# A hybrid decoder layer on one core: the triangular inverses multiplied into the keys' and outputs' operands, their rows in place of columns, and another place for the tiles between the chains

## The chip, the cores and the metric

The kernel runs on one core of one Trainium2 chip. The metric is the device time of one execution in microseconds (us). For before it is the median of three runs; the profile is of one further execution. TensorE does the matrix products, VectorE, ScalarE and GpSimd the rest, and SyncE issues most of the loads; each engine works through its own queue in order.

## The reference

One layer of a decoder over 1,024 prompt tokens and 8 x 4 sample tokens, width 1,024, float32. A Conformer convolution and an RWKV-7 time mixing run side by side on the same normed input, are merged by two sigmoid gates, and a gated MLP follows. What the change touches is the time mixing: 16 heads of 64, with the state S of 64 x 64 per head:

```python
def step(S, inp):
    r_t, w_t, k_t, a_t, b_t, v_t = inp
    sa = jnp.einsum('bhij,bhj->bhi', S, a_t)
    S = S * w_t[:, :, None, :] + sa[..., :, None] * b_t[..., None, :] + v_t[..., :, None] * k_t[..., None, :]
    y = jnp.einsum('bhij,bhj->bhi', S, r_t)
    return S, y
...
gates = jax.nn.sigmoid(zg.astype(f32))
m = gates[..., :D_MODEL] * ya.astype(f32) + gates[..., D_MODEL:] * yb.astype(f32)
```

## The kernel before

The kernel runs in four parts: the norm and the first projections (`mixer_a`), the time mixing (`mixer_b`), the merge and the output projection, and the MLP. Every large product is split into a high and a low part, so a tile of a projection is 8 x 3 products for each of three blocks of 352 tokens: 72 products of TensorE, named `mm` in the trace.

`mixer_b` cuts the prompt into chunks of 64 tokens and works on four chunks of four heads at a time, a group n of 16. Each group goes through five steps, each of them a generator:

- `prep(n)` loads keys, decays and values, and `operands(n)` writes the scaled operands E and BK.
- `stage(n)` forms the 64 x 64 lower triangles of the chunks in LQ (columns 0:64 for the inverse, 64:128 for the outputs). It inverts the 32 x 32 diagonal blocks: the blocks go to DRAM (`dL`) and come back as the tile L with one block per partition (four copies), then VectorE does 31 steps of two instructions, a product into `tm` and an addition to `X`; the result goes to DRAM (`dX`) and back into LQ. L, X and `tm` exist once (pool `lanes`).
- `combine(n)` fills the block below the diagonal with two times 16 products of 32 columns.
- `chain(n)` carries the state through its four chunks one after the other. One chunk: TensorE forms R from the state (tile `c`), VectorE copies R, TensorE multiplies by the inverse (U), VectorE scales U by `nin` into UV, TensorE multiplies by the keys BT (X), VectorE adds to the decayed state. The outputs gather in the tile `y`, which ScalarE evicts when the chain is done (`Yev`, L1173).
- `group_norm(n)` norms the outputs.

Beside them run the sample tokens, the convolution's norm (`ln_block`) and the **fillers**: 18 tiles of r, k and v, 16 tiles of gates, and at the end 8 half tiles of the convolution's output. `drive` sets the order of all this before the kernel runs: a clock counts TensorE's work at full speed, each generator yields how long it wants to wait, and while none is due the fillers emit products one by one. A group's chain waits for `combine(n)`, its stage for chain n-2, its operands for chain n-3 (three buffers). A gate is due when five or fewer have been emitted (`GATE0`) or when the chain five places back is done. The convolution's outputs start when the last chain is done (`conv_in` reuses the space of the stages). The tile framework then orders each engine's queue once more by its own schedule.

Of the kernel before, what the change touches and what calls it, by code (L numbers as in the profile page):

```python
# [7 lines left out]
F32 = mybir.dt.float32  # L8
# [23 lines left out]
class Net:  # L32
# [648 lines left out]
    def mixer_b(self):  # L681
# [4 lines left out]
        self.t_stage = {}  # L686
        self.st, self.pr, self.ch = {}, {}, {}
# [62 lines left out]
    def s_chain(self):  # L750
        for n in range(self.NH):
            yield from self.wait(("comb", n))
            yield from self.chain(n)
            self.done.add(("chain", n))
# [101 lines left out]
    GATE0 = 5  # L856

    def fillers(self):
# [5 lines left out]
        while gates or tiles or conv:  # L864
# [3 lines left out]
            if tiles:  # L868
                yield from self.rkv_tile(*tiles.pop(0))
            elif gates and due():  # L870
                yield from self.gate(*gates.pop(0))
                if not gates:
                    self.done.add("gates")
# [137 lines left out]
    def stage(self, n):  # L1011
# [4 lines left out]
        for g in range(2):  # L1016
            c4 = slice(4 * g, 4 * g + 4)
            for x in range(2):
# [7 lines left out]

                nc.gpsimd.memset(LQ[64 * x + 32:64 * x + 64, c4, 0:32], 0.0)
# [16 lines left out]
        for s in range(31):  # L1044
            a, m = s // 4 + 1, 31 - s
            tp = tm[:, :a * m].rearrange("p (a m) -> p a m", m=m)
            nc.vector.tensor_tensor(out=tp, in0=L[:, s:s + 1, s + 1:32].to_broadcast([128, a, m]),  # L1047
                                    in1=X[:, :a, s:s + 1].to_broadcast([128, a, m]), op=ALU.mult)
            nc.vector.tensor_tensor(out=X[:, :a, s + 1:32], in0=X[:, :a, s + 1:32], in1=tp, op=ALU.add)  # L1049
# [28 lines left out]
    def combine(self, n):  # L1078
# [3 lines left out]
        D11 = self.sm.tile([128, 8, 32], F32, tag="D11", name="D11", bufs=1)  # L1082
        Y21 = D11
        for x in range(2):
            nc.vector.transpose(out=D11[64 * x:64 * x + 32], in_=LQ[64 * x:64 * x + 32, :, 0:32])
        ps = self.pw_tile()
        pv = ps[:, 0:256].rearrange("p (c t) -> p c t", t=32)
        for x in range(2):
            p, q = slice(64 * x, 64 * x + 32), slice(64 * x + 32, 64 * x + 64)
            for c in range(8):  # L1090
                self.mm(pv[q, c], LQ[p, c, 32:64], D11[p, c], True, True)
        for x in range(2):
            q = slice(64 * x + 32, 64 * x + 64)
            nc.scalar.activation(out=Y21[q], in_=pv[q], func=AF.Copy)
        yield 1200
        pv = ps[:, 256:512].rearrange("p (c t) -> p c t", t=32)
        for x in range(2):
            p, q = slice(64 * x, 64 * x + 32), slice(64 * x + 32, 64 * x + 64)
            for c in range(8):
                self.mm(pv[p, c], Y21[q, c], LQ[q, c, 32:64], True, True)  # L1100
        for x in range(2):
            p = slice(64 * x, 64 * x + 32)
# [598 lines left out]
```

## Time and profile before

| | us |
|---|---|
| median of three runs | 2529.82 |
| the three runs | 2526.34, 2529.82, 2546.9 |
| the profiled execution | 2521.95 |
| its span, first to last instruction | 2520.3 |

The profile is of one execution. Times within it are us from the start of its span, which is 1.65 us shorter than the execution's own time. The trace records an f32 product as two instructions of TensorE (480 records of R's products for 15 groups of 16), and some records of products are missing, so counts of products below are taken from the built program and times from the trace. A clock of 1.00 is 2.4 GHz, one of 0.50 is 1.2 GHz; a mean between them is a mix of the two.

### The profile page before, as it was taken

The page shows a single profiled execution, that of the slowest core. Times are in us where ns is not written, and L with a number is a line of the kernel's source. Part 1 is how long each engine was busy: PE and PEld are TensorE (multiplying, and loading weights), DVE is VectorE, ACT ScalarE, POOL GpSimd, SP SyncE. Part 2 cuts the span into 40 slices and gives each one's busy share as a digit, 9 for nine tenths or more (in the row PEclk, how much of TensorE's full clock was granted, in tenths as well). Part 3 has the DMA queues.
Part 4 walks back from the last instruction along what each step waited for, and adds up shares of the span by engine and source line. Part 5 has one row for each costly group of instructions (what it writes and reads, how often), then busy time and mean ns, then how long its engine had stood idle before and what let it go on. Part 6 is the DMA issues. An engine that isn't in the chain of part 4 may idle for free.

```text
span 2520.3 us, 41895 instructions
## 1 busy us (share of the span) xinstructions
PE 2341.8 (93%) x16094; PEld 2114.6 (84%) x16094; DVE 1646.8 (65%) x4190; ACT 877.9 (35%) x1748; POOL 263.2 (10%) x562
## 2 busy tenths in 40 slices
PE   6789998987889689889999999999999999999998
PEld 5778886765668567767879999999999999999998
DVE  5999777688787877786862344475555545545556
ACT  4234333344344433543443222333232322223235
POOL 2313311011111111221221100000000000000000
PEclk9989997867679789897999999999999999999999
DMA  4124543243323332434334654431111111111111
GB/s 124 49 75 147 172 131 98 55 108 86 107 58 100 107 106 78 125 85 107 106 83 148 234 167 132 122 125 44 46 41 54 35 51 46 45 48 44 51 52 70
DMA packets 289295, 230.65 MB, mean 92 GB/s; under 512 B 82333, under 2 KB 265271, under 8 KB 288575
## 3 DMA queue, kind: packets, MB, share of 16 engines
q1 hardware_dynamic: 268615, 170.17, 24.3%
q0 software_dynamic: 20480, 57.80, 6.6%
q8 instruction: 127, 2.08, 0.4%
q14 instruction: 73, 0.60, 0.1%
HBM read 157.45 MB, written 70.45 MB: 90 GB/s over the span
## 4 chain that ended last, share of the span: by engine, by line
PE 78%; DVE 12%; DMA 6%; ACT 2%; issue 2%; SPq 1%; DVEq 0%; ACTq 0%; POOLq 0%
PE mm L54 62%; PE w L54 6%; PE c L54 2%; PE y L54 2%; DMA L<-dL 2%; DVE sg L359 2%; PE w L61 2%; DMA dX<-X 2%; DVE X L1049 1%; DVE tm L1047 1%; DVE wlo L49 1%; DMA d_ma<-ga 0%; SPq L1051 0%; DVE E L1030 0%; DVE UV L1162 0%
## 5 line engine op out<-in xcount | busy, mean ns | idle before, releaser
L54 PE MATMUL mm<-hH,whi 128*128 128x352 f32 (+1 forms) x2568 | 875.9, 341 | 14.1 <-DVE bcol L497 12.7
L54 PE MATMUL mm<-hH,wlo 128*128 128x352 f32 (+1 forms) x2568 | 851.9, 333 | 18.6 <-DVE wlo L49 18.6
L54 PE MATMUL mm<-hL,whi 128*128 128x352 f32 (+1 forms) x2568 | 854.2, 333 | 0.2 <-DVE hL L248 0.2
L54 PEld LDWEIGHTS mm<-hH,whi 128*128 128x128 f32 (+1 forms) x2568 | 491.2, 191 | 42.8 <-DVE bcol L497 14.3
L54 PEld LDWEIGHTS mm<-hH,wlo 128*128 128x128 f32 (+1 forms) x2568 | 491.6, 192 | 30.8 <-DVE wlo L49 20.8
L54 PEld LDWEIGHTS mm<-hL,whi 128*128 128x128 f32 (+1 forms) x2568 | 492.6, 192 | 11.0 <-issue 2.2
L48 ACT ACTIVATE whi<-wraw 128x1024 fp32r<-128x1024 f32 (+2 forms) x123 | 126.1, 1025 | 425.6 <-PE mm L54 340.3
L1533 DVE TENSOR_TENSOR u<-mm,rs 128x352 f32<-128x352 f32 x144 | 73.5, 511 | 225.1 <-PE mm L54 225.0
L49 DVE TENSOR_TENSOR wlo<-wraw,whi 128x1024 fp32r<-128x1024 f32 (+2 forms) x123 | 145.4, 1182 | 91.5 <-ACT whi L48 91.4
L359 DVE SCALAR_TENSOR_TENSOR sg<-cu,par,sg 128x1024 f32<-128x1024 f32 x120 | 165.4, 1382 | 1.5
L54 PE MATMUL mm<-fH,whi 128*128 128x352 f32 x504 | 163.4, 324 | 0.0
L54 PE MATMUL mm<-fH,wlo 128*128 128x352 f32 x504 | 162.8, 323 | 0.0
L54 PE MATMUL mm<-fL,whi 128*128 128x352 f32 x504 | 162.7, 323 | 0.0
L1588 DVE TENSOR_TENSOR acc<-mm,acc 128x352 f32<-128x352 f32 x168 | 86.9, 522 | 93.6 <-PE mm L54 93.6
L1563 DVE SCALAR_TENSOR_TENSOR c<-u,par,c 128x1024 f32<-128x1024 f32 x96 | 122.9, 1280 | 7.7 <-ACT c L1559 5.3
L54 PE MATMUL w<-E,BK 64*128 64x128 f32 x512 | 93.2, 332 | 32.4 <-DVE tm L1047 13.1
L54 PEld LDWEIGHTS w<-E,BK 64*128 64x128 f32 x512 | 76.5, 227 | 49.4 <-issue 27.3
L1047 DVE TENSOR_TENSOR tm<-L,X 128x60 f32<-128x60 f32 (+24 forms) x496 | 100.4, 202 | 23.6 <-DMA L<-dL 18.4
L1049 DVE TENSOR_TENSOR X<-X,tm 128x60 f32<-128x60 f32 (+24 forms) x496 | 100.4, 202 | 5.3
L54 PEld LDWEIGHTS mm<-fH,whi 128*128 128x128 f32 x504 | 94.8, 188 | 0.5
L54 PEld LDWEIGHTS mm<-fH,wlo 128*128 128x128 f32 x504 | 95.0, 188 | 0.0
L1122 ACT ACTIVATE SP<-UV,PC 64x64 f32<-64x64 f32 x192 | 64.3, 343 | 87.9 <-DVE UV L1162 78.0
(404 smaller groups left out, 3663.5 us busy)
## 6 DMA issues: line engine op xcount, KB each, us to landing
wraw<-w_in SPq DMA_DIRECT2D x50, 512.0 KB
wraw<-w_up SPq DMA_DIRECT2D x48, 512.0 KB
wraw<-w_down SPq DMA_DIRECT2D x32, 384.0 KB
L<-dL SPq DMA_DIRECT2D x16, 512.0 KB
d_alr<-la POOLq DMA_DIRECT2D x8, 528.0 KB, 3.2
d_cum<-lc POOLq DMA_DIRECT2D x8, 528.0 KB, 3.5
d_gout<-lg POOLq DMA_DIRECT2D x8, 528.0 KB, 4.0
d_k<-k POOLq DMA_DIRECT2D x24, 176.0 KB, 2.9
```

Source lines behind the costliest of these rows:

```text
L48: nc.scalar.activation(out=hi[:, :nk, :m], in_=raw[:, :nk, :m], func=AF.Copy)
L49: (lo_eng or nc.vector).tensor_tensor(out=lo[:, :nk, :m], in0=raw[:, :nk, :m], in1=hi[:, :nk, :m].bitcast(F32), op=ALU.subtract)
L54: self.nc.tensor.matmul(out, l, r, start=start, stop=stop)
L61: self.nc.tensor.transpose(out, x, ident)
L359: nc.vector.scalar_tensor_tensor(out=c[:, 0:TP], in0=u[:, t:t + TP], scalar=self.col("conv_w", t * 4 + i), in1=c[:, 0:TP], op0=ALU.mult, o ...
L1047: nc.vector.tensor_tensor(out=tp, in0=L[:, s:s + 1, s + 1:32].to_broadcast([128, a, m]), in1=X[:, :a, s:s + 1].to_broadcast([128, a, m]), ...
L1049: nc.vector.tensor_tensor(out=X[:, :a, s + 1:32], in0=X[:, :a, s + 1:32], in1=tp, op=ALU.add)
L1122: nc.scalar.activation(out=at(SP, u, x), in_=src(x)[:, u], func=AF.Copy, scale=PC[hs[x], 4 * u + c:4 * u + c + 1])
L1533: nc.vector.tensor_tensor(out=u[:, 2 + t0:2 + t0 + m], in0=p, in1=rs[:, t0:t0 + m], op=ALU.mult)
L1563: nc.vector.scalar_tensor_tensor(out=c[:, 0:TP], in0=u[:, t:t + TP], scalar=wt, in1=c[:, 0:TP], op0=ALU.mult, op1=ALU.add)
L1588: nc.vector.tensor_tensor(out=acc[i][:, s], in0=ps[:, :BW], in1=acc[i][:, s], op=ALU.add)
```

## The change

It has three parts. First, `combine` completes the inverse, multiplies it by `nin` and then multiplies it into the operands: the keys' operand BT and the outputs' half of LQ are replaced by their products with it. The chain copies R straight into UV and goes on to X; U, R0 and the products with `nin` are gone from it. The block above the diagonal is cleared by GpSimd in `combine`, where before GpSimd cleared the one below in `stage`. Second, the inverse is computed from the last row upwards, so that a step reads a column of L (32 elements apart) in place of a row; the number of elements is the same in each step of the mirrored order. Third, gates are always due, and chain n waits until min(4 + 2n, 34) filler tiles have been emitted.

```diff
+        self.filled = 0
...
         for n in range(self.NH):
             yield from self.wait(("comb", n))
+            while self.filled < min(self.FILL[0] + self.FILL[1] * n, 34):
+                yield self.POLL
...
-    GATE0 = 5
+    GATE0 = 16
+    FILL = (4, 2.0)
 
...
             if tiles:
                 yield from self.rkv_tile(*tiles.pop(0))
+                self.filled += 1
             elif gates and due():
                 yield from self.gate(*gates.pop(0))
+                self.filled += 1
...
-                nc.gpsimd.memset(LQ[64 * x + 32:64 * x + 64, c4, 0:32], 0.0)
...
-        for s in range(31):
-            a, m = s // 4 + 1, 31 - s
+
+        for s in range(31, 0, -1):
+            a, m = 8 - s // 4, s
             tp = tm[:, :a * m].rearrange("p (a m) -> p a m", m=m)
-            nc.vector.tensor_tensor(out=tp, in0=L[:, s:s + 1, s + 1:32].to_broadcast([128, a, m]),
-                                    in1=X[:, :a, s:s + 1].to_broadcast([128, a, m]), op=ALU.mult)
-            nc.vector.tensor_tensor(out=X[:, :a, s + 1:32], in0=X[:, :a, s + 1:32], in1=tp, op=ALU.add)
+            nc.vector.tensor_tensor(out=tp, in0=L[:, 0:s, s:s + 1].rearrange("p i o -> p o i").to_broadcast([128, a, m]),
+                                    in1=X[:, 8 - a:8, s:s + 1].to_broadcast([128, a, m]), op=ALU.mult)
+            nc.vector.tensor_tensor(out=X[:, 8 - a:8, 0:s], in0=X[:, 8 - a:8, 0:s], in1=tp, op=ALU.add)
...
-        D11 = self.sm.tile([128, 8, 32], F32, tag="D11", name="D11", bufs=1)
-        Y21 = D11
-        for x in range(2):
-            nc.vector.transpose(out=D11[64 * x:64 * x + 32], in_=LQ[64 * x:64 * x + 32, :, 0:32])
+        nin = self.pr[n][3]
+        hs = [slice(0, 64), slice(64, 128)]
+        lo = [slice(64 * x, 64 * x + 32) for x in range(2)]
+        up = [slice(64 * x + 32, 64 * x + 64) for x in range(2)]
+        D22 = self.sm.tile([128, 8, 32], F32, tag="D22", name="D22", bufs=1)
+        for q in up:
+            nc.vector.transpose(out=D22[q], in_=LQ[q, :, 32:64])
         ps = self.pw_tile()
         pv = ps[:, 0:256].rearrange("p (c t) -> p c t", t=32)
-        for x in range(2):
-            p, q = slice(64 * x, 64 * x + 32), slice(64 * x + 32, 64 * x + 64)
+        for p, q in zip(lo, up):
             for c in range(8):
-                self.mm(pv[q, c], LQ[p, c, 32:64], D11[p, c], True, True)
-        for x in range(2):
-            q = slice(64 * x + 32, 64 * x + 64)
-            nc.scalar.activation(out=Y21[q], in_=pv[q], func=AF.Copy)
-        yield 1200
+                self.mm(pv[q, c], LQ[p, c, 32:64], LQ[p, c, 0:32], True, True)
+        for q in up:
+            nc.scalar.activation(out=LQ[q, :, 0:32], in_=pv[q], func=AF.Copy)
+        for p in lo:
+            nc.gpsimd.memset(LQ[p, :, 32:64], 0.0)
+        yield self.W_COMB[0]
         pv = ps[:, 256:512].rearrange("p (c t) -> p c t", t=32)
-        for x in range(2):
-            p, q = slice(64 * x, 64 * x + 32), slice(64 * x + 32, 64 * x + 64)
+        for q in up:
             for c in range(8):
-                self.mm(pv[p, c], Y21[q, c], LQ[q, c, 32:64], True, True)
-        for x in range(2):
-            p = slice(64 * x, 64 * x + 32)
-            nc.scalar.activation(out=LQ[p, :, 32:64], in_=pv[p], func=AF.Copy)
-        yield 1000
+                self.mm(pv[q, c], D22[q, c], LQ[q, c, 0:32], True, True)
+        for q in up:
+            nc.scalar.activation(out=LQ[q, :, 0:32], in_=pv[q], func=AF.Copy)
+        nc.vector.tensor_tensor(out=LQ[:, :, 0:64], in0=LQ[:, :, 0:64],
+                                in1=nin[:, 0:8].rearrange("p (c o) -> p c o", o=1).to_broadcast([128, 8, 64]), op=ALU.mult)
+        for g in range(2):
+            yield self.W_COMB[1 + g]
+            ps = self.pw_tile()
+            pv = ps.rearrange("p (c t) -> p c t", t=128)
+            for c in range(4):
+                for p in hs:
+                    self.mm(pv[p, c, 0:64], LQ[p, 4 * g + c, 0:64], BT[p, 4 * g + c, p], True, True)
+                    self.mm(pv[p, c, 64:128], LQ[p, 4 * g + c, 0:64], LQ[p, 4 * g + c, 64:128], True, True)
+            for p in hs:
+                nc.scalar.activation(out=BT[p, 4 * g:4 * g + 4, p], in_=pv[p, :, 0:64], func=AF.Copy)
+            nc.scalar.activation(out=LQ[:, 4 * g:4 * g + 4, 64:128], in_=pv[:, :, 64:128], func=AF.Copy)
+        yield self.W_COMB[3]
+
+    W_COMB = (1200, 2000, 500, 1200)
 
...
-        PC, nin = self.pr[n][2:4]
+        PC = self.pr[n][2]
...
-        up = lambda t, c, x: t[hs[x], c:8:4].rearrange("p (u o) -> p u o", o=1).to_broadcast([64, 2, 64])
...
-            R0 = self.sm.tile([128, 128], F32, tag="R0", name="R0")
-            nc.vector.tensor_copy(out=R0, in_=R[:, :128])
             for u, x in ux:
                 self.mm(yo(u, x), E[x][:, 4 * u + c, 64:128], UV[:, 4 * u + c, x], c == u == 0, False)
+
+            for x in range(2):
+                nc.vector.tensor_copy(out=UV[hs[x], c:8:4, x], in_=two(R[:, :128])[hs[x]])
             yield self.LAT[0]
-            U = self.pc_tile()
-            for u, x in ux:
-                self.mm(at(U, u, x), LQ[hs[x], 4 * u + c, 0:64], at(R0, u, x), True, True)
-            for x in range(2):
-                nc.vector.tensor_tensor(out=UV[hs[x], c:8:4, x], in0=two(U[:, :128])[hs[x]], in1=up(nin, c, x), op=ALU.mult)
-            yield self.LAT[1]
             X = self.pc_tile()
             for u, x in ux:
                 self.mm(at(X, u, x), BT[:, 4 * u + c, hs[x]], UV[:, 4 * u + c, x], True, True)
...
             for u, x in ux:
...
-                yield self.LAT[2]
+                yield self.LAT[1]
...
-    LAT = (950, 1050, 1200)
+    LAT = (1200, 1500)
```

The change moves nearly everything in `mixer_b`. Two places are shown.

TensorE's queue at the end of the last chain. `c` and `y` are the chain's products, `mm<-hH` and `mm<-hL` products of a gate tile, `mm<-cs` products of the convolution's output. Before:

```order
L54 MATMUL mm<-hL,whi 128x352
L54 MATMUL mm<-hH,wlo 128x352
L54 MATMUL mm<-hH,whi 128x352
L54 MATMUL y<-UV,LQ 64x64
L54 MATMUL mm<-hL,whi 128x352
L54 MATMUL c<-UV,BK 64x64 x4
L54 MATMUL y<-UV,LQ 64x64 x3
L54 MATMUL mm<-hH,wlo 128x352
L54 MATMUL mm<-hH,whi 128x352
L54 MATMUL mm<-hL,whi 128x352
L61 MATMUL w<-ident,Sf 64x128
L54 MATMUL mm<-hH,wlo 128x352
```

After:

```order
L54 MATMUL c<-UV,E_12893 64x64
L54 MATMUL c<-UV,E_12894 64x64
L54 MATMUL c<-UV,E_12893 64x64
L54 MATMUL c<-UV,E_12894 64x64
L54 MATMUL y<-UV,E_12894 64x64
L54 MATMUL y<-UV,LQ 64x64
L54 MATMUL c<-UV,BK 64x64 x4
L54 MATMUL y<-UV,LQ 64x64 x3
L61 MATMUL w<-ident,Sf 64x128 x2
L54 MATMUL mm<-csH,whi 128x352
L54 MATMUL mm<-csL,whi 128x352
L54 MATMUL mm<-csH,wlo 128x352
```

The gate's products stand between the last chain's products and behind it before; after, the last chain's products stand alone, and the convolution's outputs follow them at once.

VectorE's queue within a chain, with the steps of another group's inverse (`tm`, `X`) between its instructions. `R<-c` and `UV<-c` are the chain's, `E` those of `operands`. Before, with the transposition of a `combine` (L1085):

```order
L1143 COPY R_6617<-c 128x128
L1047 TENSOR_TENSOR tm<-L,X 128x72
L1085 STREAM_TRANSPOSE D_6637<-LQ 32x256
L1049 TENSOR_TENSOR X<-X,tm 128x4x18
L1151 TENSOR_TENSOR UV<-c,nin 64x2x64
L1047 TENSOR_TENSOR tm<-L,X 128x68
L1151 TENSOR_TENSOR UV<-c,nin 64x2x64
L1049 TENSOR_TENSOR X<-X,tm 128x4x17
L1275 TENSOR_TENSOR sQK<-w,ms 128x64
L1047 TENSOR_TENSOR tm<-L,X 128x64
L999 TENSOR_TENSOR E_6725<-kn,P 64x8x64
```

After, with the product of LQ and `nin` of a `combine` (L1110), which waits for ScalarE and GpSimd:

```order
L1054 TENSOR_TENSOR X<-X,tm 128x6x11
L1177 SCALAR_TENSOR_TENSOR UV<-c,PC,SP 64x64
L1052 TENSOR_TENSOR tm<-L,X 128x60
L1177 SCALAR_TENSOR_TENSOR UV<-c,PC,SP 64x64
L1054 TENSOR_TENSOR X<-X,tm 128x6x10
L1110 TENSOR_TENSOR LQ<-LQ,nin 128x8x64
L1052 TENSOR_TENSOR tm<-L,X 128x54
L1166 COPY UV<-c 64x2x64
L1054 TENSOR_TENSOR X<-X,tm 128x6x9
L1166 COPY UV<-c 64x2x64
L1052 TENSOR_TENSOR tm<-L,X 128x48
L1005 TENSOR_TENSOR E_9367<-kn,P 64x8x64
```

The chain's step R (a copy) and U (two products with `nin`) has become two copies; the product with `nin` stands once per group between the steps of the inverse.

## Rows read from the trace of the kernel before

**Rows 1.** The page: busy time by engine, and three lines of the forty slices (63 us each; tenths of busy time, and of full clock).

```profile
PE 2341.8 (93%) x16094; PEld 2114.6 (84%) x16094; DVE 1646.8 (65%) x4190; ACT 877.9 (35%) x1748; POOL 263.2 (10%) x562
...
PE   6789998987889689889999999999999999999998
...
DVE  5999777688787877786862344475555545545556
...
PEclk9989997867679789897999999999999999999999
```

**Rows 2.** The instruction that evicts a chain's outputs when the chain is done (line 1173): durations least, median and most in ns, start of the first and the last.

```profile
L1173 ACT ACTIVATE Yev<-y x16: 597/597/602, 452.1 to 1321.1; 128x512 f32<-128x512 f32 x16
```

**Rows 3.** Windows of core 0: the stretch, its length, busy us and instructions of each engine, the granted clock, the DMA share and GB/s. The first is the stretch from the end of chain 0 to that of chain 15, the next seven run from one chain's end to the next one's, the last two are other stretches.

```profile
452.70:1321.70 869.00, 760.00 (x6329) 606.41 (x6329) 658.48 (x2427) 358.20 (x845) 123.97 (x267) 0.83 0.35 94
508.70:579.80 71.10, 58.76 (x453) 48.25 (x452) 54.28 (x197) 30.55 (x73) 7.76 (x21) 0.67 0.49 120
700.20:744.60 44.40, 38.46 (x361) 30.42 (x359) 38.75 (x153) 17.20 (x44) 3.30 (x8) 0.75 0.29 74
794.80:839.70 44.90, 44.90 (x353) 36.68 (x351) 35.85 (x107) 26.03 (x62) 4.76 (x12) 1.00 0.27 79
839.70:957.10 117.40, 86.60 (x583) 69.77 (x582) 91.41 (x339) 39.92 (x88) 16.75 (x38) 0.78 0.41 111
1111.70:1194.90 83.20, 73.22 (x545) 56.27 (x545) 56.25 (x199) 26.05 (x63) 11.70 (x24) 0.77 0.37 99
1194.90:1246.10 51.20, 50.63 (x488) 40.64 (x487) 41.09 (x159) 22.20 (x55) 8.01 (x16) 1.00 0.31 88
1246.10:1290.00 43.90, 43.87 (x391) 34.23 (x390) 32.76 (x126) 20.29 (x47) 13.13 (x22) 1.00 0.52 129
925.00:955.00 30.00, 30.00 (x243) 23.72 (x241) 22.52 (x89) 11.64 (x27) 4.17 (x7) 0.96 0.45 131
1404.00:1454.00 50.00, 46.35 (x281) 45.54 (x280) 26.37 (x39) 14.24 (x17) 4.26 (x8) 0.97 0.81 273
```

**Rows 4.** The inverse: its two instructions as groups of the page, the load of L and the products as the view of one line shows them (durations in ns, first and last start), and forms of the product (busy us, mean ns of one, idle time before).

```profile
L1047 DVE TENSOR_TENSOR tm<-L,X 128x60 f32<-128x60 f32 (+24 forms) x496 | 100.4, 202 | 23.6 <-DMA L<-dL 18.4
L1049 DVE TENSOR_TENSOR X<-X,tm 128x60 f32<-128x60 f32 (+24 forms) x496 | 100.4, 202 | 5.3
...
L1040 SPq DMA_DIRECT2D L<-dL x16: 557/562/617, 348.6 to 1238.5; - x16
...
L1047 DVE TENSOR_TENSOR tm<-L,X x496: 123/206/240, 358.8 to 1279.0; 128x60 f32<-128x60 f32 x16, 128x28 f32<-128x28 f32 x12, 128x66 f32<-128x66 f32 x11, 128x48 f32<-128x48 f32 x10
...
L1047 DVE TENSOR_TENSOR tm<-L,X 128x66 f32<-128x66 f32 x32 | 7.1, 222 | 0.6
...
L1047 DVE TENSOR_TENSOR tm<-L,X 128x29 f32<-128x29 f32 x16 | 2.8, 178 | 0.1
...
L1047 DVE TENSOR_TENSOR tm<-L,X 128x16 f32<-128x16 f32 x16 | 2.7, 166 | 0.2
...
L1047 DVE TENSOR_TENSOR tm<-L,X 128x8 f32<-128x8 f32 x16 | 2.6, 163 | 0.2
```

**Rows 5.** VectorE in order of time (start, us, instruction, idle time before it): the last step of an inverse and the first of the next, at two places.

```profile
766.57 0.17 DVE L1049 TENSOR_TENSOR X<-X,tm 128x8 f32<-128x8 f32 x1
...
854.93 0.19 DVE L1047 TENSOR_TENSOR tm<-L,X 128x31 f32<-128x31 f32 x1 [6.06 <-DMA L<-dL]
...
1051.37 0.17 DVE L1049 TENSOR_TENSOR X<-X,tm 128x8 f32<-128x8 f32 x1
...
1092.01 0.19 DVE L1047 TENSOR_TENSOR tm<-L,X 128x31 f32<-128x31 f32 x1 [2.89 <-DMA L<-dL]
```

**Rows 6.** Pieces of the chain that ended last, in order of time: start, us, what.

```profile
844.01 10.90 DMA L<-dL
...
893.75 10.67 DMA L<-dL
...
929.62 0.38 PE c L54 x8
...
1321.14 4.98 DMA cs<-d_cs
...
1453.26 91.98 PE mm L54 x576
```

**Rows 7.** ScalarE in order of time behind the last chain: the first instruction of the weights of four gate tiles, 1343.72 being the first and 1377.98 the fourth.

```profile
1343.72 1.06 ACT L48 ACTIVATE whi<-wraw 128x1024 fp32r<-128x1024 f32 x1 [3.22 <-DMA wraw<-w_in]
...
1377.98 1.06 ACT L48 ACTIVATE whi<-wraw 128x1024 fp32r<-128x1024 f32 x1 [3.14 <-PE mm L54]
```

**Rows 8.** Groups of instructions from 452 to 1322 us, each shape apart: busy us, mean ns of one, idle time before, and what ended it.

```profile
L1151 DVE TENSOR_TENSOR UV<-c,nin 64x128 f32<-64x128 f32 x120 | 34.4, 287 | 30.8 <-PE c L54 27.8 <-ACT whi L48 0.7
...
L1074 ACT ACTIVATE UV<-w 64x256 f32<-64x256 f32 x56 | 21.2, 378 | 10.7 <-PE w L61 9.9
...
L1143 DVE COPY R<-c 128x128 f32<-128x128 f32 x60 | 17.3, 289 | 41.0 <-PE c L54 40.4
...
L1236 DVE TENSOR_TENSOR Yev<-Yev,mu 128x512 f32<-128x512 f32 x15 | 10.2, 681 | 0.0
```

**Rows 9.** Waits from 452 to 1322 us: engine and line, who ended the wait, us in total, times, longest.

```profile
DVE R L1143 <- PE c L54: 40.4, 27, 5.5
DVE UV L1151 <- PE c L54: 27.8, 29, 6.7
...
POOL LQ L1027 <- DVE LQ L1024: 145.0, 43, 9.9
```


## The prediction

> **What bounds the kernel now.** I read the page's first two parts, then the same stretches by window, then who waited for whom, and last the forms of the instructions that the change touches. The page shows TensorE busy for 93% of the span and VectorE for 65%, and one region where that is not so: from about 340 to 1320 us many slices of TensorE fall to 6 to 8 tenths and its granted clock to 6 to 8 tenths, while VectorE stands at 6 to 8 [rows 1]. This is `mixer_b`. The sixteen chains end between 452.7 and 1321.7 us, 869 us for fifteen intervals, 57.9 us each [rows 2]. In this region TensorE is busy for 760.0 us at a mean clock of 0.83, VectorE for 658.5, ScalarE for 358.2 [rows 3]. So TensorE stands still for 109 us, and a mean of 0.83 of two levels, 2.4 and 1.2 GHz, means the lower one for a third of the time.
>
> The windows from chain end to chain end show why. Where much filler work stands between two chains (the windows that end at 839.7, 1246.1 and 1290.0), TensorE is busy throughout at a clock of 1.00 and an interval takes 43.9 to 51.2 us. Where little does (744.6), or where the next inverse is late (957.1, 1194.9), it takes 44 to 117 us at a clock of 0.75 to 0.78 [rows 3].
>
> What sets the pace there is VectorE. One inverse is 62 instructions, 200.8 us over 16 inverses, 12.55 us each [rows 4], and its buffer L exists once: the next load of L waits for the last step, and the next inverse can't start before that load has landed. The loads are issued every (1238.5 - 348.6)/15 = 59.3 us [rows 4], which is the chains' 57.9. Two of the gaps between inverses are long: 766.6 to 854.9 us and 1051.4 to 1092.0 us [rows 5]. A load takes 10.7 to 10.9 us [rows 6].
>
> Behind the last chain the order of before holds 490 filler products (6.8 gate tiles), and TensorE does them alone, with nothing else to do, at a clock of 1.00: a tile of 72 products takes (1377.98 - 1343.72)/3 = 11.42 us, 0.159 us a product [rows 7]. Then come the convolution's outputs, and the tail starts at 1453.3 us [rows 6].
>
> **The change part by part.** I make the sum against the profiled execution, 2521.95 us; the median of the three runs shown, 2529.82, lies 8 us above it.
>
> *a) The tiles in the order.* Counted in the two built orders, the products of tiles between the end of chain 0 and the end of chain 15 rise from 1612 to 2101, and those between chain 15 and the convolution's outputs fall from 490 to 0. That stretch lasts 1453.3 - 1321.7 = 131.6 us now. What stays of it is the convolution's part, 50 us (1404 to 1454 [rows 3]), and the load of its operand, which the gates hide now and nothing hides then: 4.98 us [rows 6] plus some 3 us for the split and the first product. 131.6 - 58 = **-74 us**. Bounds: -82 if the load is hidden after all, -64 if the 50 us begin at half clock and with both loads late.
>
> The 490 products themselves go among the chains. They cost 490 x 0.159 = 78 us of TensorE at full clock. The cover is TensorE's 109 us of idle time and its half clock, together far more than 78. If that cover is gone, the price is rival 1.
>
> *b) Folding.* Per group TensorE loses 16 products of 64 columns (U) and gains 32 (16 for the keys, 16 for the outputs). Four such products, eight records in the trace, take 0.38 us [rows 6] in a window with a clock of 0.96 [rows 3], so 0.095 each: 16 x 0.095 x 16 groups = 24 us, also put into the idle time (0 there, 48 at half clock and uncovered). ScalarE gains four evictions of 64x256 (0.378 each) and two of 128x256, taken at 0.5: 2.5 us a group, 40 us in all on an engine that is busy for 358 of 869 us: nothing. VectorE loses the copy of R (64 x 0.289 = 18.5 us) and gains one product of 128x512 per group (16 x 0.681 = 10.9 us); the two copies into UV stand for the two products of before (0.287 against 0.289, nothing) [rows 8]. Net -7.6 us; it is in the VectorE sums of c). GpSimd's 64 clearings become 32 larger ones.
>
> The added wait: VectorE's product of LQ with nin now waits for ScalarE's second eviction and for GpSimd's clearing, and behind it stand the steps of the running inverse and the copies of the running chain. GpSimd waited long for others in front of just such clearings (145 us in total, 9.9 at most [rows 9]), because its queue is in order. Where it is late, inverse and chain stop together. Between 0 and 16 x 2 us; the order puts the two clearings directly behind DMA issues that belong to tiles further up, so I take 0 and keep 30 for the range.
>
> *c) VectorE's loop.* I took the order of VectorE in both programs and gave every instruction its form's mean from the trace. Between the last step of one inverse and the first of the next there is other work for 5 to 9 us in eleven of fifteen gaps before, 14 to 15 us in two, 26 and 69 us in the two long ones. After: 7 to 9 us in seven gaps, 17 to 31 us in eight. A gap can't be shorter than the load with its issue, 12 us. With that the gaps sum to 256 us before and 259 after. Inside the inverses other work sums to 408 us before and 384 after. With 201 us for the inverses' own steps: 865 us before, 844 after, **-21 us**. The trace has 358.8 to 1279.0 us for it [rows 4] and a last step behind, 921 us, so 56 us are waits on others, which I keep.
>
> *d) The shorter chain.* VectorE waits 40.4 us before the copies of R and 27.8 before the products with nin [rows 9]. The round of 27.8 us goes away; what is late next is the product X behind the same copies, and TensorE is fuller, so I take **-10 us** (0 to -28).
>
> *e) Rows of the inverses.* The element count is the same (1,560 per inverse), but the steps read a column of L, 32 elements apart. No row reads so many elements so; the nearest is the 128x8 form of the step's product, whose second input lies 32 apart: 163 ns, where the line through 128x29 (178) and 128x66 (222) gives 153 [rows 4]. That is 10 ns for 8 elements, 1.25 each: at most 1.25 x 1,560 x 16 = 31 us; at least 0, as the 10 ns can be the floor of a form so small. I take **+5 us**, nearer to the floor, because the form of 16 elements, two in a run, stands at 166 already [rows 4].
>
> The Trainium skill, page "Advanced Engine Details and Errata", section "SBUF Cachelines", says that full speed wants two hits on each 16-byte line and that a stride which takes a new line for every element is penalised. It gives no figure; an estimate of one more element time each, (222 - 178)/37 = 1.2 ns x 1,560 x 16 = 30 us, would make the sum 2447 instead of 2422. The trace of before leaves both open: the 10 ns above would agree with it.
>
> Sum: -74 - 21 - 10 + 5 = -100 us, 2521.95 - 100 = **2422 us**.
>
> **The rivals.** *1. Slower: TensorE becomes the bound.* The place is the stretch between chains: 78 + 24 = 102 us of new work on an engine in order, where a tile in front of a chain's product delays VectorE and a late VectorE stops the tiles. If nothing is absorbed and the clock stays at 0.83, the region grows by 102/0.83 = 123 us: 2522 - 74 + 123 = 2571 us. It decides from 62.9 us per chain on ((869 + 74)/15). For it: the intervals to 579.8 and 744.6, with 1.2 and 0.7 tiles between the chains by the order, already take 71.1 and 44.4 us, at clocks of 0.67 and 0.75. Against it: the dense ones take 43.9 to 51.2 us without a pause [rows 3]. The Trainium skill, page "TensorE: Matmul & The Clock Gate", section "HAM oscillation — how this bites in real kernels", tells that bursts with pauses between them lose the clock anew each time. The windows here agree where the pauses are (0.67 with 12 us of idle time before 579.8) and show 1.00 where tiles fill them.
>
> *2. Much faster: the region runs like its dense intervals.* VectorE's 658.5 us are 43.9 per chain; at 85% busy, as in the window to 1246.1 (41.1 of 51.2), that is 52 us, 780 us in all: -89 instead of -26, 2359 us. For it: no gap before an inverse holds over 31 us of other work any more. Against it: in c) the other work still stands inside the inverses.
>
> *3. Nothing: a part of the moved work comes back.* If the region grows by as much as the stretch behind it shrinks, 74 of the 102 us uncovered, the time stays at 2522 us: the tiles have changed their place and nothing else. For it: TensorE's idle time lies in many short waits between TensorE and VectorE (27 of them make up the 40.4 us before R [rows 9]), into which a tile's products fit only where the order puts them. Against it: 74 us is 4.9 per chain, and VectorE alone is idle for (869 - 658.5)/15 = 14 per chain.
>
> **How the numbers follow.** My forecast, 2385 to 2465 us, has 0.52; rival 2 has 0.20, rival 3 0.16, rival 1 0.12. A measurement tells about 1% from no change here, 25 us around 2529.82. Faster by over 1% (under 2505) are the forecast, rival 2 and half of rival 3: 0.80. Within 1%: 0.09, the other half of rival 3 and a little of rival 1. Slower: 0.11. The range leaves out rival 1, the upper part of rival 3 and the fast end of rival 2: 2350 to 2515. It holds the bounds of a) to e): from -82 - 21 - 28 = -131 (2391) to -64 + 0 + 0 + 31 + 30 = -3 (2519, of which the last 4 us are left out).
>
> **What would show it.** Right: the last chain's end is followed within 60 us by the tail; the chains' ends lie 54 to 58 us apart on average; the granted clock of the region is above 0.9; the gaps before inverses 8 and 12 are under 40 us; the wait before the old product with nin is gone and no longer wait takes its place on VectorE. Wrong in a): gate tiles or idle time of over 20 us behind the last chain. Wrong in b) and d): GpSimd's clearing or ScalarE's eviction as what ends VectorE's longest waits. Wrong in c): chains further apart than 62.9 us. Wrong in e): a mean of the steps' products above 225 ns, where it is 202 now.

## The result, and the profile after

The changed kernel takes 2507.01 us (median of 19 runs), the kernel before, run beside it, 2532.89: a ratio of 0.9893, 95% interval 0.987 to 0.9917. It is faster by 26 us where 100 were forecast. The profiled execution took 2528.8 us, 22 above the median, and its stretch of the chains is long by about as much: up to the end of the eleventh interval between chains it takes 740.0 us, where experiment 4 takes 716.6 for the same number of instructions of TensorE.

The page of the changed kernel, with the lines of [rows 1]:

```profile
PE 2352.6 (93%) x16606; PEld 2147.9 (85%) x16606; DVE 1662.5 (66%) x4144; ACT 914.0 (36%) x1846; POOL 259.8 (10%) x528
...
PE   6889988988988889989998899999999999999998
...
DVE  5999866887677886667685544466555545545556
...
PEclk9989996987877987889799899999999999999999
```

The weak stretch of TensorE and of its clock is still there, and it ends later: before the convolution's outputs the last digit under 9 is the 18th of TensorE and the 19th of its clock before, the 22nd and the 20th now (the 23rd holds the start of those outputs). The chains' ends, as in [rows 2], then windows as in [rows 3] (length, busy us and instructions of PE, PEld, DVE, ACT and POOL, clock, DMA share, GB/s): all chains, two intervals between chains, a stretch at the lower clock, the stretch behind the last chain:

```profile
L1188 ACT ACTIVATE Yev<-y x16: 580/597/598, 461.7 to 1399.1; 128x512 f32<-128x512 f32 x16
```

```profile
462.30:1399.70 937.40, 836.48 (x7295) 705.17 (x7293) 689.17 (x2398) 415.44 (x973) 134.26 (x265) 0.83 0.36 98
1202.30:1270.90 68.60, 64.02 (x534) 52.61 (x534) 46.23 (x157) 26.61 (x63) 10.97 (x20) 0.78 0.36 98
1270.90:1325.90 55.00, 52.53 (x532) 43.73 (x533) 47.28 (x160) 25.85 (x62) 11.80 (x21) 1.00 0.41 101
544.30:561.40 17.10, 12.62 (x48) 10.47 (x48) 16.21 (x69) 4.82 (x10) 2.24 (x5) 0.50 0.12 30
1399.70:1525.00 125.30, 115.09 (x702) 113.31 (x703) 59.31 (x108) 28.10 (x42) 4.94 (x9) 0.95 0.64 194
```

The fifteen intervals take 937.4 us in place of 869.0: in the two profiles the 68 us more are nearly what left the end. With the 22 us by which this execution lies above its median taken off, an estimate, it is 46 us; 71 us less behind the last chain (below) and 46 more before it leave 25, close to the 26 gained. TensorE is busy for 76 us more, stands idle for 101 us where it stood for 109, and its mean clock is 0.83 as before. Behind the last chain the tail now starts after 61 us (132 before), here in the chain that ended last:

```profile
1460.88 91.83 PE mm L54 x576
```

The inverse, as in [rows 4], and VectorE's waits between 462 and 1400 us, as in [rows 9]:

```profile
L1052 DVE TENSOR_TENSOR tm<-L,X 128x60 f32<-128x60 f32 (+24 forms) x496 | 116.1, 234 | 47.4 <-DMA L<-dL 41.4
...
L1054 DVE TENSOR_TENSOR X<-X,tm 128x60 f32<-128x60 f32 (+24 forms) x496 | 101.5, 205 | 6.3
```

```profile
L1052 DVE TENSOR_TENSOR tm<-L,X 128x66 f32<-128x66 f32 x32 | 8.4, 262 | 0.4
...
L1052 DVE TENSOR_TENSOR tm<-L,X 128x29 f32<-128x29 f32 x16 | 3.2, 201 | 0.3
L1052 DVE TENSOR_TENSOR tm<-L,X 128x8 f32<-128x8 f32 x16 | 2.7, 168 | 0.2
```

```profile
DVE tm L1052 <- DMA L<-dL: 36.6, 9, 7.2
DVE UV L1177 <- PE c L54: 25.9, 19, 5.1
DVE UV L1166 <- PE y L54: 25.8, 13, 6.3
...
DVE LQ L1110 <- ACT LQ L1109: 12.5, 6, 3.1
...
DVE UV L1166 <- PE c L54: 9.7, 6, 3.7
```

The wait before the product with `nin` (27.8 us) is gone, and another stands in its place: the copy of R into UV (L1166) waits for products **y**. The four products that form the outputs from the state read UV; the copy overwrites that state, so it must wait until they have read it. Before, R went into R0 and these products lay beside the copy.

One reading is used for all experiments. A run's span and mean clock split it in two: F = span x clock, H = 2 x (span - F) is the time at the lower clock, and span = F + H/2. It is a way of counting and no cause: F holds the time at full clock and half of that at the lower one, and pauses count in it like work. Within one kernel's runs F moves little: 18 runs of the changed kernel have F from 2317 to 2331 and H from 328 to 399. One at 2490.2 us (span 2488.5, clock 0.934) and one at 2523.9 (2522.2, 0.921) have F 2324 and 2323, H 328 and 399; the clock has three digits, so F is good to 1.3 us. Runs over 1.5% above the fastest of their kernel are left out of F, H and the ratios.

### The profile page after: what moved, and what is told of

Its sections match the earlier page's. It is cut to its first block, busy times and chain, and to the rows that moved or that the text cites. A ratio compares the mean times of both kernels' runs of the same rounds, so it can differ in the third digit from the quotient of the medians.

```text
span 2527.1 us, 42949 instructions
## 1 busy us (share of the span) xinstructions
PE 2352.6 (93%) x16606; PEld 2147.9 (85%) x16606; DVE 1662.5 (66%) x4144; ACT 914.0 (36%) x1846; POOL 259.8 (10%) x528
## 4 chain that ended last, share of the span: by engine, by line
PE 55%; DVE 11%; DMA 7%; issue 2%; ACT 1%; SPq 0%; POOL 0%; DVEq 0%; ACTq 0%; POOLq 0%
PE mm L54 47%; PE w L54 4%; DMA L<-dL 3%; PE y L54 1%; DVE tm L1052 1%; PE c L54 1%; DVE X L1054 1%; DVE E L1034 1%; PE w L61 1%; DMA d_ma<-ga 1%; DMA ga<-d_ga 1%; DVE BK L1008 0%; DMA sl<-state_wkv 0%; DVE LQ L1030 0%; DVE BK L1007 0%
## 5 line engine op out<-in xcount | busy, mean ns | idle before, releaser
L54 PEld LDWEIGHTS mm<-hH,whi 128*128 128x128 f32 (+1 forms) x2568 | 496.9, 194 | 42.3 <-issue 12.5
L54 PEld LDWEIGHTS mm<-hH,wlo 128*128 128x128 f32 (+1 forms) x2568 | 497.7, 194 | 21.2 <-DVE wlo L49 12.3
L54 PEld LDWEIGHTS mm<-hL,whi 128*128 128x128 f32 (+1 forms) x2568 | 498.5, 194 | 9.1 <-issue 1.5
L1052 DVE TENSOR_TENSOR tm<-L,X 128x60 f32<-128x60 f32 (+24 forms) x496 | 116.1, 234 | 47.4 <-DMA L<-dL 41.4
L54 PE MATMUL w<-E,BK 64*128 64x128 f32 x512 | 88.9, 329 | 31.9 <-DVE BK L1008 15.7
```

The lines of the kernel that those rows point to most:

```text
L54: self.nc.tensor.matmul(out, l, r, start=start, stop=stop)
L1052: nc.vector.tensor_tensor(out=tp, in0=L[:, 0:s, s:s + 1].rearrange("p i o -> p o i").to_broadcast([128, a, m]), in1=X[:, 8 - a:8, s:s + 1] ...
```

## The experiments

Ratios are to runs of the kernel before taken beside each experiment, with 95% intervals, and where ratios and medians tell different sizes both are given; F and H are means over the runs, in us. Each edit also shifts a few neighbours in the built order.

| kernel | median | ratio | F | H |
|---|---|---|---|---|
| before | 2533 | 1 | 2334 | 398 |
| changed | 2507 | 0.9893 [0.987, 0.9917] | 2323 | 367 |
| 1 order only | 2483 | 0.9789 [0.974, 0.9837] | 2318 | 328 |
| 2 fold only | 2562 | 1.0089 [1.0058, 1.0121] | 2349 | 420 |
| 3 row read | 2499 | 0.9828 [0.9781, 0.9875] | 2317 | 362 |
| 4 few products | 2488 | 0.9812 [0.9769, 0.9854] | 2267 | 442 |
| 5 two homes | 2484 | 0.9787 [0.9738, 0.9837] | 2318 | 330 |
| 6 double fold | 2499 | 0.9863 [0.9819, 0.9907] | 2350 | 297 |
| 7 clearing on VectorE | 2528 | 0.9992 [0.9963, 1.0022] | 2328 | 397 |
| 8 order, columns | 2489 | 0.9797 [0.9742, 0.9851] | 2323 | 317 |
| 9 fold only, two homes | 2546 | 1.0038 [1.0009, 1.0067] | 2351 | 385 |
| 10 nudged | 2505 | 0.9875 [0.9838, 0.9913] | 2320 | 364 |
| 11 order, late tiles | 2547 | 1.0056 [1.0025, 1.0087] | 2332 | 430 |
| 12 two homes, late tiles | 2504 | 0.9881 [0.9845, 0.9918] | 2327 | 353 |
| 13 two homes, useless products | 2546 | 1.0036 [1.0007, 1.0066] | 2387 | 317 |
| 14 two homes, longer delays | 2479 | 0.9779 [0.9738, 0.9819] | 2309 | 337 |
| 15 two homes, 6 + 2n | 2486 | 0.9799 [0.9764, 0.9834] | 2323 | 322 |

**1 and 2: the parts apart.** The first puts the rule (`GATE0 = 16`, `FILL`, the chain's wait) into the kernel before; the second takes it out of the changed one:

```diff
-    GATE0 = 16
-    FILL = (4, 2.0)
+    GATE0 = 5
+    FILL = (0, 0.0)
```

> The kernel before with the new order rule alone (chains wait for 4 + 2n tiles, gates always due); inverses, chain and combine as before. Theory P (TensorE pays for the moved tiles: neither its waits nor its half clock shrink when tiles come in): the stretch behind the last chain loses 70 to 75 us and the region of the chains gains as much, 2515 to 2550 us. Rival F (the folding eats the gain of the order): the order alone gives most of what was forecast, 2440 to 2475 us.

> The changed kernel with the order rule of before (no wait of the chains for tiles, five gate tiles before the first chain): folding and rows of the inverses alone. Theory P: a shorter chain and a lighter VectorE loop are worth 10 to 35 us, 2495 to 2520 us, with the tail of tiles behind the last chain as before. Rival F: 16 products more per group, the wait of the product with nin and the strided reading cost more than the chain gains, 2545 to 2570 us.

The order alone is worth 53 us (2533 x 0.0211), twice the whole change; the folding with its rows costs 23 us alone and 26 on top of the order (0.9893 against 0.9789). Theory P falls in both. Rival F's range holds in 2; in 1 the 2483 us lie 8 above it. Order only, all chains:

```profile
459.40:1361.80 902.40, 824.95 (x6779) 674.47 (x6778) 674.37 (x2433) 379.90 (x880) 134.29 (x286) 0.86 0.37 100
```

The same stretch cut behind its eleventh interval, in the kernel before and with the order only:

```profile
452.70:1111.70 659.00, 560.57 (x4599) 451.82 (x4599) 510.96 (x1893) 274.84 (x646) 86.26 (x197) 0.81 0.34 93
1111.70:1321.70 210.00, 199.43 (x1732) 154.60 (x1732) 147.52 (x535) 83.36 (x199) 37.71 (x70) 0.91 0.36 96
```

```profile
459.40:1173.00 713.60, 649.50 (x5196) 530.06 (x5196) 536.74 (x1962) 294.65 (x685) 102.31 (x226) 0.85 0.37 98
1173.00:1361.80 188.80, 175.44 (x1585) 144.41 (x1583) 137.62 (x472) 85.26 (x196) 31.97 (x60) 0.89 0.37 107
```

The traces have 1,148 products of tiles in the first eleven intervals before and 1,597 with the new order. The 449 more would take 71 us at full clock (0.159 us each); the eleven intervals grow by 55. TensorE's idle time there falls from 98 to 64 us and H from 253 to 214, while F rises from 533 to 606: most of the moved work came in as time. These are single executions. How far the lengths can be off shows in the changed kernel and experiment 4, which differ by 23 us over the same instructions up to there (740.0 and 716.6); their F is 607 and 611. The last four intervals hold as many such products as before (464 and 465) and are 21 us shorter; no run shows why.

**3 and 8: rows or columns.** In 3 the step of the changed kernel reads `L[:, 31 - s:32 - s, 32 - s:32]`; in 8 that of kernel 1 reads `L[:, 0:31 - s, 31 - s:32 - s]`, a column.

> The changed kernel, but the steps of the inverse read a row of L in place of a column (so the inverses are other numbers; all else is the same). Theory P: the inverses end 40 us before their chains start, so 16 us less on VectorE are worth 0 to 8 us, 2500 to 2510 us; the steps' products come back from 234 to 202 ns. Rival S (the strided read delays VectorE, and with it the copies of the chains): 16 to 30 us, 2475 to 2490 us.

> The first experiment's kernel (order rule alone), but its inverses read a column of L in place of a row (other numbers; all else the same). Theory S (the strided reading costs its time wherever the inverse stands): the steps' products go from 202 to 234 ns, 16 us of VectorE, and the time rises by 8 to 16 us, 2491 to 2499 us. Theory P: the inverses are hidden, within 5 us of 2483 us.

By the medians it is 8 us one way and 6 the other, by the ratios 16 and 2, and the intervals overlap both times: the strided read costs between nothing and its 16 us, and does not explain the folding's 26. With the row read the steps' products take 204 ns again (234 in the changed kernel).

**4: what a tile's product costs.**

```diff
-        yield from self.project_g(w, (self.hH, self.hL), 8, ev)
+        yield from self.project_g(w, (self.hH, self.hL), 8 if 8 * x + i < 9 else 1, ev)
```

> The changed kernel with one eighth of the products in the last seven gate tiles (441 of 504 left out; their loads, evictions and stores stay). Theory P: the time falls by their whole price, 60 to 85 us, to 2420 to 2450 us. Rival L (the region is paced by the chains' latency and by VectorE, and the tiles stand in TensorE's idle time): the time stays within 15 us of the changed kernel's 2507.

20 us, outside both ranges and nearer to rival L's. F falls by 56 us, but H rises by 75. The last four intervals, with 27 to 52 such products in two and none in the others, where the changed kernel has 520 in all:

```profile
1168.90:1354.40 185.50, 139.21 (x1263) 107.32 (x1261) 135.43 (x445) 93.15 (x219) 33.05 (x60) 0.66 0.41 111
```

```profile
1202.30:1399.70 197.40, 181.15 (x1704) 153.68 (x1702) 139.50 (x444) 94.60 (x217) 34.61 (x62) 0.88 0.38 107
```

Without tiles TensorE works and waits at a clock of 0.66; with them the stretch is 12 us longer at 0.88. So in these four intervals the cover for the tiles exists, up to about two per chain. Of the first eleven, where the order put its 449 more, this experiment says nothing.

**5, 9 and 10: the copy's wait.** In 5 R goes into a tile of its own:

```diff
+            UW = self.sm.tile([128, 2, 2, 64], F32, tag="UW", name="UW", bufs=1)
+            for x in range(2):
+                nc.scalar.activation(out=UW[hs[1 - x], :, x], in_=UV[hs[1 - x], c:8:4, x], func=AF.Copy)
             for x in range(2):
-                nc.vector.tensor_copy(out=UV[hs[x], c:8:4, x], in_=two(R[:, :128])[hs[x]])
+                nc.vector.tensor_copy(out=UW[hs[x], :, x], in_=two(R[:, :128])[hs[x]])
```

and X and the last output products read UW. 9 does the same in kernel 2; 10 sets `LAT` to (1150, 1550).

> The changed kernel, but R goes into a tile of its own beside a copy of V (ScalarE makes that copy, two of 64x128 per chunk), so that VectorE's copy no longer overwrites the state which the output's products still read. Theory W (the folding put the output's four products on the chain: the copies stand idle for 45.8 us, 27.9 of them behind those products): 15 to 30 us off the changed kernel's 2507, to 2477 to 2492 us, and the wait of the copy for y is gone. Rival K (the price is the folding's own products and evictions): 2500 to 2515 us.

> The second experiment's kernel (folding and rows of the inverses, the order rule of before) with R in a tile of its own as in the fifth. Theory W (the copy's wait for the output's products is the folding's price, in whatever order): 20 to 35 us off that kernel's ratio of 1.009, so 0.995 to 1.001, 2520 to 2540 us. Rival N (the fifth experiment's gain was luck of the built order): within 10 us of the second's 2562 us.

> The changed kernel with the planner's two delays in the chain set to 1150 and 1550 in place of 1200 and 1500: the same work, about an eighth of TensorE's rows a place or two further up or down. It measures what such shifts are worth by themselves. Theories W and J's opposite (the clearing on VectorE cost 21 us by its wait): within 8 us of 2507 us. Rival N: 15 us or more away from it, in either direction.

Theory W holds in the new order: 27 us by the ratios (23 by the medians), most of it in H (367 to 330). In the old one it is 13 us, between the two answers expected (its ratio of 1.0038 is 3 thousandths above W's), and the intervals of 2 and 9 overlap. Shifting the order by itself is worth 2 us (5 by the ratios). VectorE's waits in 5 between 450 and 1400 us no longer have y in front of the copy (L1169):

```profile
DVE tm L1052 <- DMA L<-dL: 32.9, 7, 7.8
DVE UW L1169 <- PE c L54: 31.9, 20, 4.6
DVE UV L1180 <- PE c L54: 20.0, 19, 3.0
```

From the end of a chunk's last product R to its first product X the 64 chunks take 451.5 us in the changed kernel, 453.6 in 10, 419.9 in 5 and 420.0 in 14. These 32 us answer to the 27.

**6 and 7: the folding's work and the clearing.** In 6 the 32 products and 6 evictions of each group are made twice; in 7 the clearing is `nc.vector.memset`.

> The changed kernel with the 32 products and 6 evictions that the folding has per group made twice (the same values to the same places; the order's clock does not count the second set). Rival K: the second set costs what the first one does, 32 x 0.095 x 16 = 49 us of TensorE and 16 x 2.5 = 40 us of ScalarE, in the path from the inverse to the chain: 30 to 50 us, 2537 to 2557 us. Theory W: most of it is hidden, at most 15 us, 2507 to 2522 us.

> The changed kernel with the two clearings of LQ in the combining on VectorE in place of GpSimd, whose in-order queue waited 87 us in front of them. Theory J (those waits hold up the stores of tiles and with them the tiles' buffers): 10 to 25 us faster, 2482 to 2497 us, and 32 instructions of some 0.2 us more on VectorE. Theories W and K: within 6 us of 2507 us.

Doubling costs nothing: F rises by 27, H falls by 70. K falls. Moving the clearing answers none of the theories: it costs 21 us (25 by the ratios), H by 30 and F by 5 more. One of its twelve runs, 2542.2 us at a clock of 0.868, has F 2205 and H 671, far from the other eleven, and is not in these means. J falls: a GpSimd freed of the clearing brought no gain, while VectorE now waits for the products that read the block:

```profile
DVE LQ L1102 <- PE w L54: 11.0, 5, 5.7
```

**11, 12 and 15: another rule for the tiles.** `FILL[0] + FILL[1] * n + FILL[2] * n * n` with (4, 1.3, 0.047) in 11 and 12; (6, 2.0) without the last term in 15.

> The first experiment's kernel with another rule: chain n waits for 4 + 1.3n + 0.047n^2 tiles (20.7 for chain 9 in place of 22, 34 for the last as before). Theory T (a tile product costs 0.12 us between the first eleven chains and 0.03 between the last four, so tiles are better late): 5 to 15 us faster than its 2483, to 2468 to 2478 us. Rival P: no difference beyond 5 us.

> The fifth experiment's kernel (R in a tile of its own) with the rule of the eleventh. Theory T: 5 to 15 us faster than the fifth's 2484, to 2469 to 2479 us. Rival P: no difference beyond 5 us.

> The fifth experiment's kernel with chains that wait for 6 + 2n tiles in place of 4 + 2n. Theory C (tiles hold the clock early as well as late, and a spread of two per chain counts, not where it begins): within 8 us of 2484 us. Rival E (the early chains have too few tiles, as the 11th experiment with still fewer was 64 us slower): 10 to 25 us faster, 2459 to 2474 us.

Theory T had the sign wrong: 11 is 64 us slower than 1 and 12 is 20 slower than 5, outside rival P's 5 as well. Two intervals of 11, the first with 36 products of tiles, half a tile, the second with 153:

```profile
537.70:595.20 57.50, 40.37 (x264) 31.05 (x263) 40.50 (x140) 19.37 (x47) 8.57 (x21) 0.61 0.36 88
595.20:686.80 91.60, 76.49 (x638) 62.64 (x638) 62.87 (x255) 33.53 (x81) 8.15 (x18) 0.81 0.24 65
```

An early interval with hardly any tiles loses the clock. Over all, the first eleven intervals have 193 products fewer than in 1 (1,404) and are no shorter (718.0 us for 713.6), while the last four have 191 more (656) and are 37 us longer (225.5 for 188.8):

```profile
466.20:1184.20 718.00, 626.04 (x5005) 504.52 (x5004) 535.43 (x1969) 288.81 (x674) 98.15 (x218) 0.82 0.35 93
1184.20:1409.70 225.50, 202.89 (x1775) 171.96 (x1773) 144.36 (x465) 91.85 (x207) 36.33 (x68) 0.90 0.37 103
```

Where the even spread of two per chain begins makes no difference (15), as theory C expected there.

**13 and 14: the clock as a cause.** 13 adds useless products to 5, 14 sets `LAT` to (1800, 2200).

```diff
+            for _ in range(2):
+                nc.tensor.matmul(R[:, 256:384], self.ident, self.ident, start=True, stop=True)
             yield self.LAT[0]
```

> The fifth experiment's kernel with two useless products of 128x128 behind the products R and two behind the products X of each chunk (identity by identity, into the free columns of the same bank): 256 products, at full clock 256 x 0.21 = 55 us of TensorE. Theory C (the time at half clock is the loss, and it comes from stretches in which TensorE waits in a chain): the half clock falls by 60 to 140 us, and the time stays within 20 us of 2484 us or falls. Rival B (TensorE is the bound and its work costs its time): 2530 to 2550 us.

> The fifth experiment's kernel with the planner's delays in the chain at 1800 and 2200 in place of 1200 and 1500, so that more of the tiles' products stand in the waits of a chain and fewer between chains. Theory C: less time at half clock, 5 to 25 us faster, 2460 to 2480 us. Rival B: the chains get longer and nothing else, 2484 to 2500 us.

Useless products cost 62 us: F rises by 69, H falls by 13. In the trace they keep TensorE busy for 95.8 us, not for the 55 expected:

```profile
L1189 PE MATMUL c<-ident 128*128 128x128 f32 x256 | 48.3, 316 | 8.5 <-DVE UV L1182 5.5 <-DVE Sf L1182 2.9
L1171 PE MATMUL c<-ident 128*128 128x128 f32 x256 | 47.5, 314 | 2.9 <-DVE UW L1169 2.6
```

Theory C falls for work in the chains themselves. The folding's doubled products brought H down by 70 instead. They too stand in the chains for the most part: 1,664 of their 2,048 records in the trace lie between a chain's first R and the eviction of its outputs. Why the two differ is not settled. 14 is 5 us faster than 5, inside the intervals, and in theory C's range, but H did not fall (337 for 330). It beats both kernels at 0.9779, but 1, 5, 8, 14 and 15 can't be told apart.

## Why the prediction was right and wrong

*Where the 74 us went that were forecast and did not come.* By the ratios, 21 are in step a): the order brought 53 of its 74 us. The other 53 are in the folding with its rows: -26 was forecast for c), d) and e) together, and on top of the order they cost 26. Of these 53 us 27 are the wait that step d) had not seen, and about 26 are gains of c) and d) that stayed out, with what the strided read cost above its +5. That 2507 us lies inside the range of 2350 to 2515 is luck: the sum behind its slow end (a late load, the wait of LQ x `nin`, the full price of the strided read) holds neither of the two causes that the experiments found, tiles that were not covered and the copy's wait.

*Direction, and what stood behind the last chain: right.* The tail starts 61 us behind the last chain (58 forecast). From the last chain's end to the end of the span it is 1127.4 us in place of 1198.6: -71 against -74.

*Step a), "together far more than 78": a step that failed, in its size.* Of the 74 us the order alone keeps 53. The cover was booked as idle time plus half clock, as if the tiles would use up both. In the first eleven intervals, where they were put, 71 us of tiles made the stretch 55 us longer (experiment 1). Over all fifteen F went from 724 to 774 us, TensorE's idle time from 109 to 77 and H from 290 to 257, where "above 0.9" asked for an H of less than 0.2 x 869 = 174. In the changed kernel's profile F is 781 and H 313, the clock 0.83. So idle time and half clock gave way by a part of themselves and not by the whole; what bounds that part is not shown. The page "TensorE: Matmul & The Clock Gate", section "HAM oscillation — how this bites in real kernels", of the Trainium skill tells of pauses that lose the clock anew. The trace agrees where the pauses are (0.61 with 17 us of idle time in experiment 11), and two tiles per chain did not remove them.

*Step b), "taken as hidden": right for its products and evictions.* Doubled, they cost nothing (6). The added wait of LQ x `nin` is there (12.5 us for ScalarE, taken as 0, 30 for the range) and no run prices it alone; GpSimd's clearing does not end VectorE's long waits.

*Step d), the shorter chain, -10: the step that failed most, wrong in sign by a wait that I did not see.* I wrote "what is late next is the product X behind the same copies" and overlooked that the copies write into the tile that the output's products read. It costs 27 us (5) and stands at 25.8 us on VectorE. Without it the folding is worth 0 (0.9787 against 0.9789) and not -10, though the stretch from R to X falls from 622.8 us in kernel 1 to 419.9 in 5, 203 us in all. Most of it comes back between chains: from one chain's end to the next one's first R there are 8.2 us on average in kernel 1 and 19.0 in 5 (3.1 before, 17.0 in the changed kernel), and the interval is 60.2 and 60.7 us. F is 2318 in both. With the old order the stretch hardly falls at all (645.2 before, 607.5 in 9). That the chain now waits for its tiles on TensorE, and no longer on its rounds, is how I read it; no run takes that wait away without changing the order, and the cause stays open.

*Step c), VectorE's loop sets the pace, -21: in the new order it no longer does.* In the changed kernel the inverses of chains 1 to 15 end 33 to 93 us before their chains' first R. Inverse 10, for one, has ended and its combining starts at 1042.8 us; its chain's first R comes at 1103.2. With the old order (9) the first R comes at most 31 us behind the inverse's end, but the loop did not get shorter: the loads of L are (1281.8 - 350.2)/15 = 62.1 us apart, not closer than the 59.3 of [rows 4], and the two long gaps are still there (94 and 49 us). The 12 us that a gap was to take at least was too much as well: eight of the fifteen gaps of before are shorter, down to 9.6 us.

*Step e), +5, 0 to 31: inside its bounds, three times its size on VectorE, and above the 225 ns named.* The steps' products take 234 ns in place of 202, 15.7 us in all: 0.6 to 0.8 ns more per element (262 against 222 at 66, 201 against 178 at 29). So the section "SBUF Cachelines" of the Trainium skill's "Advanced Engine Details and Errata" agrees with the trace that such a stride is penalised; the price on this form is half of the estimate made from it. In the kernel's time it is 0 to 16 us (3, 8).

*The rivals.* Rival 3 came nearest (part of the moved work comes back), but its cause is only a part: with the copy's wait removed 54 of the 100 us are there. Rival 1 was wrong for the last four intervals, as experiment 4 shows (441 products, 70 us at full clock, cost 20), near the mark for the first eleven (55 of 71 us in 1) and right for work put into the chains (13). Of the signs named, the tail was missed by 1 us (61 for 60); the chains' distance (62.5 us for 54 to 58), the clock and the wait that took the place of the one before `nin` spoke against the forecast, and of the gaps before inverses 8 and 12 one is over 40 us (46) and one under it (13).

## What to carry to other kernels

When a copy is redirected into the tile that a product reads, list every other reader of what it overwrites: a buffer saved can put work that lay beside the path onto it. TensorE's idle time and its half clock are no account from which moved work can be paid twice; split each run into F and the time at the lower clock and see which of the two an edit moves, and price the moved work in the stretch where it was put. Test a change of three parts part by part: here one part alone was worth twice the whole (0.9789 for 0.9893).

## What the runs showed of the hardware

Tile products taken away can lower the clock of what stays: 441 fewer gave back 56 us of F and took 37 as half clock (H + 75), and the four intervals that lost them ran at 0.66 in place of 0.88. The same clearings, 32 instructions, moved from GpSimd to VectorE added 30 us of time at the lower clock and 5 of F. A product of VectorE that reads one operand 128 bytes apart took 262 ns in place of 222 for 66 elements and 201 in place of 178 for 29. And two runs of one program differ by 34 us (2490 and 2524) with F equal within 1 us, H from 328 to 399: the spread between these runs is the clock's.
